# Second product of both MLPs as Strassen's seven products of halves

## The chip, the cores and the metric

The kernel runs on one core of one Trainium2 chip. The metric is device time in microseconds of one execution. A core has five engines that run their own instruction queues in order: TensorE (matmuls, PE in the profile, with PEld for its weight loads), VectorE (DVE), ScalarE (ACT), GpSimd (POOL) and SyncE (SP, which here only issues transfers). SBUF is the on-chip memory of 128 partitions; PSUM holds what TensorE accumulates, in banks of 512 float32 columns per partition.

## The reference

Two transformer blocks over 512 tokens of width 1024, in float32. The first has a hybrid mixer (gated spatial mixing and a gated delta rule), cross attention to 256 memory rows and an MLP; the second has an mLSTM and sliding window attention with gates, an MLP, and a gated per-layer embedding. What matters here are the two MLPs:

```
def squared_relu_mlp(h, w1, w2):                 # block 1: w1 1024x4096, w2 4096x1024
    return jnp.square(jax.nn.relu(h @ w1)) @ w2
...
u = rmsnorm_2(x, norm_mlp_g[i]) @ w_up[i]        # block 2, the same sizes
x = x + jnp.square(jax.nn.relu(u)) @ w_down[i]
```

## The kernel before

**Layout.** Activations are kept feature-major: a tile is 128 features by 512 tokens. The residual `x` is `self.x`, [128, 8, 512], and stays in SBUF. Other large operands lie in numbered slots `S0` to `S12` of 8 KB per partition (`slot`, line 86): 0 to 8 in a pool that lives through the whole kernel, 9 to 12 in one opened for a part of it.

**Precision.** Every float32 product is three matmuls (`mm3`, line 217). Each operand is split in a high part, rounded by ScalarE, and a low part, the rest, subtracted by VectorE (`split_sb` line 257, for weights `wload` line 193, the two instructions of which are lines 203 and 204); high x high, high x low and low x high are accumulated in the same PSUM bank.

**Weights.** A granule is 256 output columns of 1024 input rows. `wgran` (line 207) loads it in two halves of [128, 4, 256], 512 KB each, over SP (line 200) into `wr` (two buffers), and splits them into `wh` and `wl` (three buffers each), all in the pool `wp` that is opened at line 70 and never closed. The layout on the host (`gran`, line 311) makes each half one contiguous piece per partition.

**Product.** `proj_fm` (line 224) takes a granule and for each of its two output tiles runs 8 x 3 matmuls with a 128x128 weight tile as the stationary operand and 512 token columns as the moving one, into one of three PSUM banks `psd`, and calls a function that evacuates the bank. `proj_tm` exchanges the roles: 256 weight columns move.

**The MLP.** `ffn` (line 792) divides the 4096 hidden features in four quarters. `up(q)` makes eight hidden tiles with four granules of the first weight: VectorE applies relu and the norm's factor (line 804), ScalarE squares (line 805), and the tile is split into its high and low slots (lines 261 and 262). `down(q)` takes four granules of the second weight and adds to `x` (`add_res`, line 401). The order is up(0), up(1), down(0), up(2), down(1), up(3), down(2), down(3), with two sets of four slots for the hidden tiles. In the last quarter the evacuation also prepares the next stage, tile by tile: a scaled split of `x` (lines 264 and 265) and sums of squares, squared by ScalarE and added by GpSimd (line 276), one such sum after the second MLP and two after the first (`between`, line 829; `tail`, line 1184).

**Order.** The program is written as data flow over tiles in pools. A planner puts each engine's instructions in a fixed order beforehand: by their place in the program, but an instruction whose inputs and buffers are expected to be ready may go ahead of one that still waits. It adds the semaphores. A pool that is closed gives its memory to pools opened later; pools are placed one above another.

Of the kernel before, what the change touches and what calls it, by code (L numbers as in the profile page):

```python
# [2 lines left out]

# [1 line left out]

# [59 lines left out]
class Kern:  # L65
    def __init__(self, tc, ctx, D, out, dbg=None):
        self.tc, self.nc, self.ctx, self.D, self.out = tc, tc.nc, ctx, D, out
        self.dbg = dbg or {}
        self.const = ctx.enter_context(tc.tile_pool(name="const", bufs=1))
        self.wp = ctx.enter_context(tc.tile_pool(name="wp", bufs=3))  # L70
        self.sp = ctx.enter_context(tc.tile_pool(name="sp", bufs=1))
        self.tp = ctx.enter_context(tc.tile_pool(name="tp", bufs=2))
        self.pd = ctx.enter_context(tc.tile_pool(name="pd", bufs=3, space=PSUM))
        self.ps = ctx.enter_context(tc.tile_pool(name="ps", bufs=1, space=PSUM))
        self.n = 0
# [8 lines left out]


    def slot(self, i, shape, dt=F32):
        return (self.sp if i < 9 else self.sp2).tile(shape, dt, tag=f"S{i}", name=self.uid(f"S{i}"))

    def t(self, pool, shape, tag, dt=F32, bufs=None):
# [82 lines left out]
    def softplus(self, pool, z, n, tag):  # L172
# [16 lines left out]
        nc.vector.scalar_tensor_tensor(out=a, in0=a, scalar=2.0, in1=s, op0=ALU.mult, op1=ALU.add)  # L189
        return a  # L190


    def wload(self, src, kt, n, pieces=None):

# [19 lines left out]
        lo = [parts[k // 4][1][:, k % 4] for k in range(nk)]  # L214
        return hi, lo

    def mm3(self, ps, ah, al, bh, bl, first, last):

        mm = self.nc.tensor.matmul
        mm(ps, ah, bh, start=first, stop=False)  # L220
        mm(ps, ah, bl, start=False, stop=False)  # L221
        mm(ps, al, bh, start=False, stop=last)  # L222

    def proj_fm(self, w, xh, xl, tiles, evac, ncol=T, pool=None):
        wh, wl = w
# [500 lines left out]
    def xattn(self, xh, xl, acc, mem):  # L726
        nc = self.nc
        kh, kl, vh, vl = mem
        rs = self.tok_rs(acc, "rs")
        ident = self.mask("ident")  # L730
        oh, ol = [], []
        with self.tc.tile_pool(name="xa", bufs=2) as xp, self.psums() as self.pc:
# [4 lines left out]
            for h in range(4):  # L737
                q = self.slot((0, 1, 7, 4)[h], [P, 4, T], F32R)
# [7 lines left out]
                for t2 in range(2):  # L746
                    ps = self.psc("sc").rearrange("p (i m) -> p i m", i=2)
                    for i in range(2):
                        c = slice((2 * t2 + i) * P, (2 * t2 + i + 1) * P)
# [5 lines left out]
                    p = self.t(xp, [P, 2, 256], "p")  # L755
# [23 lines left out]
        xh, xl = self.pair((9, 10)), self.pair((11, 12))  # L779
        acc = self.new_acc()  # L780

        def ev(o, ps):
# [6 lines left out]
        return xh, xl, acc  # L789


    def ffn(self, w1, w2, xh, xl, acc, evac):
        nc = self.nc
        rs = self.tok_rs(acc, "rs")
        bc = self.tok_bc(rs, "bc")
        H = {}

        def up(q):
            s = (0, 1, 2, 3) if q % 2 == 0 else (4, 5, 6, 7)
            hh, hl = self.pair(s[:2]), self.pair(s[2:])  # L800

            def ev(o, ps):
                t = self.t(self.tp, [P, T], "e1")
                nc.vector.scalar_tensor_tensor(out=t, in0=ps, scalar=0.0, in1=bc, op0=ALU.max, op1=ALU.mult)  # L804
                nc.scalar.activation(t, t, AF.Square)  # L805
                self.split_sb(hh[o], hl[o], t)

            for g in range(4):
                self.proj_fm(self.wgran(w1, 4 * q + g), xh, xl, (2 * g, 2 * g + 1), ev)
            H[q] = hh, hl  # L810

        def down(q, ev):
            for g in range(4):
                self.proj_fm(self.wgran2(w2, 4 * q + g), *H[q], (2 * g, 2 * g + 1), ev)

        up(0)
        up(1)
        down(0, self.add_res)
        up(2)
        down(1, self.add_res)  # L820
        up(3)
        down(2, self.add_res)
        down(3, evac)

    def wgran2(self, name, g):
        return self.wgran(name, g)


    def between(self):

        nc = self.nc
        g12 = self.t(self.tp, [P, KT], "g12", bufs=1)
        c1, c2 = VCOL["norm_final"], VCOL["norm_mix_g_2"]
        nc.vector.tensor_tensor(out=g12, in0=self.vec[:, c1:c1 + 8], in1=self.vec[:, c2:c2 + 8], op=ALU.mult)
        xh, xl = self.pair((0, 1)), self.pair((2, 3))
        acc, acc2 = self.new_acc(), None

        def ev(o, ps):
            nonlocal acc2
            if o == 0:  # L840
                acc2 = self.slot(9, [P, T])
            self.add_res(o, ps)
            self.split_sb(xh[o], xl[o], self.x[:, o], g12[:, o:o + 1])
            self.sq_acc(acc, self.x[:, o], o)
            self.sq_acc(acc2, self.x[:, o], o, scale=self.vcol("norm_final", o))

        def fin():
            self.dump("x3", self.x)
            r1 = self.tok_rs(acc, "rs")
# [333 lines left out]

    def tail(self):
        nc = self.nc
        xh, xl = self.pair((0, 1)), self.pair((2, 3))
        acc = self.new_acc()

        def ev(o, ps):
            self.add_res(o, ps)  # L1190
            self.norm_tile(o, xh, xl, acc, "norm_ple_g_2")

        def ple():
            self.dump("x6", self.x)
            raw = self.slot(9, [P, 2, T])
            nc.sync.dma_start(raw, self.D["p"])
            ph = self.slot(10, [P, 4, T], F32R)
            for i in range(2):
                self.split_sb(ph[:, i], ph[:, 2 + i], raw[:, i])
            pp = [self.slot(i, [P, 4, T]) for i in (11, 12)]  # L1200

            def ev_p(o, ps):
                nc.scalar.copy(pp[o // 4][:, o % 4], ps)
# [27 lines left out]
            sq = self.slot(9, [P, 2, 2, 256])  # L1231
            y = self.slot(10, [P, 2, 1024])
            one = self.ones[:, 0:1]
            with self.psums() as self.pc:

# [18 lines left out]
                r0 = stat(0)  # L1254
# [12 lines left out]
                ps = self.pss()  # L1267
# [13 lines left out]
def body(tc, D, out, dbg=None):  # L1281
    with ExitStack() as ctx:
        K = Kern(tc, ctx, D, out, dbg)
        K.setup()
        K.mixer()
        mem = K.memory()
        with tc.tile_pool(name="sp2", bufs=1) as K.sp2:
            op = K.w_out1()
            op = K.xattn(*op, mem)
            ev, fin = K.between()  # L1290
            K.ffn("ffn_w1", "ffn_w2", *op, ev)
            op2 = fin()
        mh, ml = K.mixer2(*op2)
        with tc.tile_pool(name="sp3", bufs=1) as K.sp2:
            xh, xl = K.pair((9, 10)), K.pair((11, 12))
# [8 lines left out]
            K.dump("x5", K.x)  # L1304
            ev, ple = K.tail()
            K.ffn("w_up_2", "w_down_2", xh, xl, acc, ev)
            ple()


# [1 line left out]
def gran(w, n=256):  # L1311

    kk, nn = w.shape
    return np.ascontiguousarray(w.reshape(kk // 512, 4, P, nn // n, n).transpose(3, 0, 2, 1, 4))


def fm(a):
# [8 lines left out]
def layout(i):  # L1326
# [21 lines left out]
        o["w_ple_gate" if n == "w_ple_gate_2" else n] = gran(sq(n))  # L1348
    for n in ("ffn_w2", "w_down_2"):
        w = sq(n)  # L1350
        o[n] = np.ascontiguousarray(np.concatenate([gran(w[1024 * q:1024 * q + 1024]) for q in range(4)], axis=0))
# [31 lines left out]
```

## Time and profile before

| | us |
|---|---|
| median of 3 runs (lowest, highest) | 1758.17 (1754.64, 1764.05) |
| the profiled execution | 1758.89 |
| its span, first to last instruction | 1757.1 |
| TensorE busy, matmuls | 1719.7 (8740 instructions) |
| VectorE busy | 1011.4 (2039) |
| ScalarE busy | 720.9 (1254) |
| GpSimd busy | 148.4 (126) |

The granted TensorE clock was 0.992 over the span. Busy times of successive instructions overlap: a matmul of 512 columns is shown with 0.39 us, while the next starts 0.23 us after it. So a price of TensorE or VectorE work is read from the distance between starts. The two MLPs take about 0.36 ms each: the evacuations of `up` (line 804) run from 461.2 to 1594.7 us over both, and the first MLP's weights are loaded from 432.3 us on, its last tile of `x` added at 811.1 us. A row of the timeline holds the start, the duration, the engine, the line, the operation, output and input, and in brackets how long the engine stood idle before it and what ended that. A row of the table by stage holds for each stretch its length and then busy time and count of PE, PEld, DVE, ACT and POOL, the granted clock, the DMA share and GB/s.

### The profile page before, as it was taken

The page shows a single profiled execution, that of the slowest core. Times are in us where ns is not written, and L with a number is a line of the kernel's source. Part 1 is how long each engine was busy: PE and PEld are TensorE (multiplying, and loading weights), DVE is VectorE, ACT ScalarE, POOL GpSimd, SP SyncE. Part 2 cuts the span into 40 slices and gives each one's busy share as a digit, 9 for nine tenths or more (in the row PEclk, how much of TensorE's full clock was granted, in tenths as well). Part 3 has the DMA queues.
Part 4 walks back from the last instruction along what each step waited for, and adds up shares of the span by engine and source line. Part 5 has one row for each costly group of instructions (what it writes and reads, how often), then busy time and mean ns, then how long its engine had stood idle before and what let it go on. Part 6 is the DMA issues. An engine that isn't in the chain of part 4 may idle for free.

```text
span 1757.1 us, 22629 instructions
## 1 busy us (share of the span) xinstructions
PE 1719.7 (98%) x8740; PEld 1427.2 (81%) x8740; DVE 1011.4 (58%) x2039; ACT 720.9 (41%) x1254; POOL 148.4 (8%) x126
## 2 busy tenths in 40 slices
PE   7999999999999999999999999999999999999997
PEld 6987788877888888888888887788888888888886
DVE  6898886655543444446755469865555434344446
ACT  5344444444333333334444448654234323232343
POOL 2211321201000000012000000000120000000112
PEclk9999998999999999999999999999999999999999
DMA  5221232312222223223222321223222222323231
GB/s 196 88 72 61 71 97 77 118 51 72 96 97 96 93 89 95 95 86 95 73 73 74 95 73 49 72 73 96 86 97 89 91 95 96 96 96 108 90 102 61
DMA packets 49436, 155.09 MB, mean 88 GB/s; under 512 B 9392, under 2 KB 11696, under 8 KB 49328
## 3 DMA queue, kind: packets, MB, share of 16 engines
q1 hardware_dynamic: 49328, 153.64, 27.4%
q8 instruction: 69, 1.13, 0.3%
q14 instruction: 39, 0.32, 0.1%
HBM read 151.26 MB, written 2.10 MB: 87 GB/s over the span
## 4 chain that ended last, share of the span: by engine, by line
PE 87%; DVE 9%; ACT 2%; issue 2%; DMA 0%; POOL 0%; SPq 0%; DVEq 0%; ACTq 0%
PE psd L221 26%; PE psd L222 26%; PE psd L220 26%; DVE wl L204 1%; PE c L563 1%; ACT wh L203 1%; PE lg L1147 1%; PE po L1174 1%; PE c L512 1%; PE m L1068 1%; DVE S L368 1%; DVE e L319 1%; PE pss L1169 0%; PE m L1076 0%; DVE dA L583 0%
## 5 line engine op out<-in xcount | busy, mean ns | idle before, releaser
L220 PE MATMUL psd<-S,wh 128*128 128x512 f32 (+1 forms) x1968 | 770.5, 392 | 6.3 <-ACT wh L203 6.3
L222 PE MATMUL psd<-S,wl 128*128 128x512 f32 (+1 forms) x1968 | 774.3, 394 | 1.3 <-DVE wl L204 1.3
L221 PE MATMUL psd<-S,wh 128*128 128x512 f32 (+1 forms) x1904 | 748.1, 393 | 2.4 <-DVE S L265 2.3
L204 DVE TENSOR_TENSOR wl<-wr,wh 128x1024 fp32r<-128x1024 f32 (+3 forms) x281 | 349.4, 1243 | 227.0 <-ACT wh L203 225.9
L203 ACT CAST wh<-wr 128x1024 fp32r<-128x1024 f32 (+3 forms) x281 | 292.0, 1039 | 434.3 <-PE psd L221 406.5
L220 PEld LDWEIGHTS psd<-S,wh 128*128 128x128 f32 x1968 | 372.7, 189 | 86.2 <-ACT wh L203 7.2
L222 PEld LDWEIGHTS psd<-S,wl 128*128 128x128 f32 x1968 | 371.5, 189 | 79.8 <-DVE wl L204 2.3
L221 PEld LDWEIGHTS psd<-S,wh 128*128 128x128 f32 x1904 | 358.7, 188 | 80.6 <-DVE S L265 4.2
L276 POOL TENSOR_TENSOR acc<-acc,sq 128x512 f32<-128x512 f32 (+1 forms) x47 | 67.9, 1446 | 916.8 <-ACT sq L274 916.3
L401 DVE TENSOR_TENSOR x_fm<-psd,x_fm 128x512 f32<-128x512 f32 x88 | 60.7, 690 | 137.8 <-PE psd L222 137.7
L221 PE MATMUL psd<-wl,S 128*128 128x256 f32 (+2 forms) x480 | 137.4, 286 | 0.6 <-DVE wl L204 0.6
L222 PE MATMUL psd<-wh,S 128*128 128x256 f32 (+2 forms) x480 | 137.1, 286 | 0.0
L220 PE MATMUL psd<-wh,S 128*128 128x256 f32 (+2 forms) x480 | 136.5, 284 | 0.0
L804 DVE SCALAR_TENSOR_TENSOR e<-psd,bc 128x512 f32<-128x512 f32 x64 | 44.3, 691 | 112.2 <-PE psd L222 109.3
L805 ACT ACTIVATE e<-e 128x512 f32<-128x512 f32 x64 | 40.4, 632 | 135.1 <-DVE e L804 135.1
L221 PEld LDWEIGHTS psd<-wl,S 128*128 128x128 f32 x480 | 91.6, 191 | 1.4 <-DVE wl L204 1.0
L220 PEld LDWEIGHTS psd<-wh,S 128*128 128x128 f32 x480 | 91.8, 191 | 0.4
L222 PEld LDWEIGHTS psd<-wh,S 128*128 128x128 f32 x480 | 91.8, 191 | 0.1
L262 DVE TENSOR_TENSOR S<-e,S 128x512 fp32r<-128x512 f32 (+1 forms) x84 | 56.7, 675 | 49.2 <-ACT S L261 49.2
L261 ACT CAST S<-e 128x512 fp32r<-128x512 f32 (+1 forms) x84 | 50.5, 601 | 42.9 <-POOL e L931 27.1
L264 ACT ACTIVATE S<-x_fm,vec 128x512 fp32r<-128x512 f32 x40 | 28.9, 721 | 55.4 <-DVE x_fm L401 36.9
L319 DVE SCALAR_TENSOR_TENSOR e<-e,vec,e 128x511 f32<-128x511 f32 (+2 forms) x60 | 46.6, 779 | 2.6 <-ACT e L316 2.2
(411 smaller groups left out, 1459.7 us busy)
## 6 DMA issues: line engine op xcount, KB each, us to landing
wr<-in_ffn_w_dram SPq DMA_DIRECT2D x64, 512.0 KB
wr<-in_w_up_dram SPq DMA_DIRECT2D x32, 512.0 KB
wr<-in_w_down_dram SPq DMA_DIRECT2D x32, 512.0 KB
wr<-in_w_in_qk_dram SPq DMA_DIRECT2D x16, 512.0 KB
wr<-in_w_in_v_dram SPq DMA_DIRECT2D x12, 512.0 KB
wr<-in_xa_wk_dram SPq DMA_DIRECT2D x8, 512.0 KB
wr<-in_xa_wv_dram SPq DMA_DIRECT2D x8, 512.0 KB
wr<-in_xa_wq_dram SPq DMA_DIRECT2D x8, 512.0 KB
```

The lines of the kernel that those rows point to most:

```text
L203: nc.scalar.copy(hi[:, c], raw[:, c])
L204: nc.vector.tensor_tensor(out=lo[:, c], in0=raw[:, c], in1=hi[:, c].bitcast(F32), op=ALU.subtract)
L220: mm(ps, ah, bh, start=first, stop=False)
L221: mm(ps, ah, bl, start=False, stop=False)
L222: mm(ps, al, bh, start=False, stop=last)
L261: nc.scalar.copy(hi, src)
L262: nc.vector.tensor_tensor(out=lo, in0=src, in1=hi.bitcast(F32), op=ALU.subtract)
L276: eng.tensor_tensor(out=acc, in0=acc, in1=sq, op=ALU.add)
L319: nc.vector.scalar_tensor_tensor(out=c[:, s:], in0=xr[:, :T - s], scalar=w(j), in1=c[:, s:], op0=ALU.mult, op1=ALU.add)
L401: self.nc.vector.tensor_tensor(out=self.x[:, o], in0=ps, in1=self.x[:, o], op=ALU.add)
L804: nc.vector.scalar_tensor_tensor(out=t, in0=ps, scalar=0.0, in1=bc, op0=ALU.max, op1=ALU.mult)
L805: nc.scalar.activation(t, t, AF.Square)
```

## The change

`down` no longer multiplies a granule as a whole. The granule's 1024 x 256 weights are four blocks, two halves of the input tiles (even and odd ones) by two halves of the output columns; the hidden quarter is likewise two halves of the features by two halves of the tokens (256 each). Strassen's scheme in Winograd's form computes the four blocks of the result with seven products of such halves instead of eight, each of 4 x 3 matmuls with 256 moving columns. It needs four sums of weight blocks and four sums of hidden blocks, each split like any operand.

- `st_weights` loads the four raw blocks in three transfers, makes the four sums on VectorE and splits seven blocks, in three pieces of 1024 columns and one of 512.
- `st_fill` is called after each `up` granule: it makes the four hidden sums on VectorE (`ms`), and splits seven pieces of 256 columns in four steps. `st_operand` takes seven slots for them.
- `st_gemm` runs the seven products in the PSUM banks X, Z (a new pool of four banks, `px`) and Y (a bank of `psd`), and adds after each product to the block of `x` that needs it: products 3, 5 and 6 accumulate on top of what is in X, product 4 on Z.
- `ffn` runs the quarters in the order up(0), down(0), up(1), down(1), and so on. After a granule of the last quarter `post` does for its two tiles what the evacuation did before.
- The weight pool is no longer one: `weights()` opens it with three buffers for everything else and with five for each MLP (the second to the end of the kernel). Slots are renumbered to fit (`perm`), and a pool `fp` holds what is used in an MLP only. `halves` lays the second weights out on the host, without arithmetic.

```
-        self.wp = ctx.enter_context(tc.tile_pool(name="wp", bufs=3))
...
+    @contextmanager
+    def weights(self, bufs=3):
+        with self.tc.tile_pool(name=self.uid("wp"), bufs=bufs) as self.wp:
+            yield
...
+    def st_fill(self, H, k, e1, e2):
...
+        h = (slice(0, 256), slice(256, 512))
+        ms = self.t(self.fp, [P, 4, 256], "ms", bufs=1)
+        TT(out=ms[:, 3], in0=e2[:, h[1]], in1=e1[:, h[1]], op=ALU.subtract)
+        TT(out=ms[:, 1], in0=e1[:, h[0]], in1=e1[:, h[1]], op=ALU.subtract)
+        STT(out=ms[:, 2], in0=ms[:, 3], scalar=-1.0, in1=e1[:, h[0]], op0=ALU.mult, op1=ALU.subtract)
+        STT(out=ms[:, 0], in0=ms[:, 2], scalar=-1.0, in1=e2[:, h[0]], op0=ALU.mult, op1=ALU.subtract)
+        self.split_sb(t[6][:, 0, k], t[6][:, 1, k], e1[:, h[0]])
+        self.split_sb(t[4][:, :, k], t[5][:, :, k], e2.rearrange("p (a c) -> p a c", a=2))
+        self.split_sb(t[2][:, :, k], t[3][:, :, k], ms[:, 2:4])
+        self.split_sb(t[0][:, :, k], t[1][:, :, k], ms[:, 0:2])
...
+    def st_weights(self, src):
...
+        nc.sync.dma_start(r0, src[:, 0:2])
+        nc.sync.dma_start(r1, src[:, 2:3])
+        nc.sync.dma_start(r2, src[:, 3:4])
...
+        split(r0)
+        nc.vector.tensor_tensor(out=ss[:, 0], in0=r0[:, 0], in1=r2[:, 0], op=ALU.add)
+        nc.vector.tensor_tensor(out=ss[:, 1], in0=r1[:, 0], in1=r2[:, 0], op=ALU.add)
+        split(ss)
+        s2 = self.t(self.wp, [P, 2, T], "ws2", bufs=1)
+        nc.vector.tensor_tensor(out=s2[:, 0], in0=ss[:, 0], in1=r1[:, 0], op=ALU.add)
+        nc.vector.tensor_tensor(out=s2[:, 1], in0=s2[:, 0], in1=r0[:, 1], op=ALU.add)
+        split(s2)
+        split(r1)
+        a11, a12, s3, s1, s2, s4, a22 = out
+        return a11, a12, s1, s2, s4, s3, a22
+
+    def st_gemm(self, src, H, o1, post):
...
+        def prod(i, ps, m, first):
+            ah, al = w[i]
+            for k in range(4):
+                c = slice(k * P, (k + 1) * P)
+                self.mm3(ps, ah[:, c], al[:, c], hi[m][:, k], lo[m][:, k], first and k == 0, k == 3, not first)
+
+        def add(n, t, ps, op=ALU.add):
+            TT(out=x[n][t], in0=x[n][t], in1=ps, op=op)
+
+        prod(0, X, 0, True)
+        add(0, 0, X)
+        prod(1, Y, 1, True)
+        add(0, 0, Y)
+        prod(2, Z, 4, True)
+        add(1, 1, Z, ALU.subtract)
+        prod(3, X, 5, False)
+        add(0, 1, X)
+        prod(4, Z, 2, False)
+        add(0, 1, Z)
+        prod(5, X, 6, False)
+        add(1, 1, X, ALU.subtract)
+        prod(6, X, 3, False)
+        add(1, 0, X, ALU.subtract)
+        for o in (o1, o1 + 1):
+            post(o)
...
+            for q in range(4):
+                H = None
+                for g in range(4):
...
+                    self.proj_fm(self.wgran(w1, 4 * q + g), xh, xl, (2 * g, 2 * g + 1), ev)
+                    H = H or self.st_operand(slots)
+                    self.st_fill(H, g, *es)
+                for g in range(4):
+                    self.st_gemm(self.D[w2][4 * q + g], H, 2 * g, post if q == 3 else lambda o: None)
...
-        K.setup()
...
+        with K.weights():
+            K.setup()
+            K.mixer()
+            mem = K.memory()
...
+        with K.weights(5), tc.tile_pool(name="fp", bufs=1) as K.fp:
+            K.sp2 = K.fp
             ev, fin = K.between()
...
+            K.ffn("ffn_w1", "ffn_w2", *op, (0, 1, 4, 7, 8, 9, 10), ev)
             op2 = fin()
...
+        with K.weights():
+            K.perm = [2, 3, 5, 6, 0, 1, 4, 7, 8]
+            mh, ml = K.mixer2(*op2)
...
+        with K.weights(5), tc.tile_pool(name="fp", bufs=1) as K.fp:
...
+            K.ffn("w_up_2", "w_down_2", xh, xl, acc, (2, 3, 5, 6, 8, 9, 10), ev)
```

More of the change, by code (lines that the diff above doesn't have):

```diff
@@ L1 @@
 import math
-from contextlib import ExitStack
+from contextlib import ExitStack, contextmanager
 import numpy as np
@@ L215, in wgran, with mm3 @@
         return hi, lo
-    def mm3(self, ps, ah, al, bh, bl, first, last):
+    def mm3(self, ps, ah, al, bh, bl, first, last, more=False):
         mm = self.nc.tensor.matmul
-        mm(ps, ah, bh, start=first, stop=False)
-        mm(ps, ah, bl, start=False, stop=False)
-        mm(ps, al, bh, start=False, stop=last)
+        mm(ps, ah, bh, start=first, stop=False, skip_group_check=more)
+        mm(ps, ah, bl, start=False, stop=False, skip_group_check=more)
+        mm(ps, al, bh, start=False, stop=last, skip_group_check=more)
     def proj_fm(self, w, xh, xl, tiles, evac, ncol=T, pool=None):
@@ L778, in xattn @@
                     ol.append(O[:, 2 + o])
-        xh, xl = self.pair((9, 10)), self.pair((11, 12))
+        xh, xl = self.pair((2, 3)), self.pair((5, 6))
         acc = self.new_acc()
@@ L789, in xattn @@
         return xh, xl, acc
-    def ffn(self, w1, w2, xh, xl, acc, evac):
-        nc = self.nc
[L794 to L823, printed above, removed]
@@ new lines, in st_weights, with split @@
+    def st_weights(self, src):
+        nc = self.nc
+        r0 = self.t(self.wp, [P, 2, T], "wr", bufs=2)
+        r1 = self.t(self.wp, [P, 1, T], "wr1", bufs=2)
+        ss = self.t(self.wp, [P, 2, T], "ws", bufs=1)
+        r2 = self.t(self.wp, [P, 1, T], "wr2", bufs=2)
+        nc.sync.dma_start(r0, src[:, 0:2])
+        nc.sync.dma_start(r1, src[:, 2:3])
+        nc.sync.dma_start(r2, src[:, 3:4])
+        out = []
+        def split(raw):
+            n = raw.shape[1]
+            hi, lo = self.t(self.wp, [P, n, T], "wh", F32R), self.t(self.wp, [P, n, T], "wl", F32R)
+            self.split_sb(hi, lo, raw)
+            out.extend((hi[:, i], lo[:, i]) for i in range(n))
+        split(r0)
[9 more added lines that the diff above has]
+        return a11, a12, s1, s2, s4, s3, a22
@@ new lines, in st_gemm @@
+    def st_gemm(self, src, H, o1, post):
+        nc = self.nc
+        TT = nc.vector.tensor_tensor
+        w = self.st_weights(src)
+        _, hi, lo = H
+        X, Z = (self.t(self.px, [P, T], "x")[:, :256] for _ in range(2))
+        Y = self.psd()[:, :256]
+        x = [[self.x[:, o1 + n, t * 256:t * 256 + 256] for t in range(2)] for n in range(2)]
+        def prod(i, ps, m, first):
[21 more added lines that the diff above has]
+            post(o)
@@ L834, in between, with ev @@
         nc.vector.tensor_tensor(out=g12, in0=self.vec[:, c1:c1 + 8], in1=self.vec[:, c2:c2 + 8], op=ALU.mult)
[L835 to L839, printed above, removed]
+        ops = None
+        def ev(o):
+            nonlocal ops
             if o == 0:
-                acc2 = self.slot(9, [P, T])
-            self.add_res(o, ps)
+                ops = self.pair((2, 3)), self.pair((5, 6)), self.new_acc(), self.t(self.fp, [P, T], "acc2", bufs=1)
+            xh, xl, acc, acc2 = ops
             self.split_sb(xh[o], xl[o], self.x[:, o], g12[:, o:o + 1])
@@ L1185, in tail, with ev @@
         nc = self.nc
[L1186 to L1191, printed above, removed]
+        raw = self.t(self.fp, [P, 2, T], "p", bufs=1)
+        nc.sync.dma_start(raw, self.D["p"])
+        ops = None
+        def ev(o):
+            nonlocal ops
+            if o == 0:
+                ops = self.pair((0, 1)), self.pair((4, 7)), self.new_acc()
+            self.norm_tile(o, *ops, "norm_ple_g_2")
         def ple():
+            xh, xl, acc = ops
             self.dump("x6", self.x)
-            raw = self.slot(9, [P, 2, T])
-            nc.sync.dma_start(raw, self.D["p"])
-            ph = self.slot(10, [P, 4, T], F32R)
+            ph = self.slot(8, [P, 4, T], F32R)
             for i in range(2):
                 self.split_sb(ph[:, i], ph[:, 2 + i], raw[:, i])
-            pp = [self.slot(i, [P, 4, T]) for i in (11, 12)]
+            pp = [self.slot(i, [P, 4, T]) for i in (2, 3)]
             def ev_p(o, ps):
@@ L1230, in ple @@
             wh, wl = self.wgran("w_ple_gate", 3)
[L1231 to L1232 removed]
+            sq = self.slot(5, [P, 2, 2, 256])
+            y = self.slot(6, [P, 2, 1024])
             one = self.ones[:, 0:1]
@@ L1283, in body @@
         K = Kern(tc, ctx, D, out, dbg)
-        K.setup()
[L1285 to L1289, printed above, removed]
+        with K.weights():
+            K.setup()
+            K.mixer()
+            mem = K.memory()
+            with tc.tile_pool(name="sp2", bufs=1) as K.sp2:
+                op = K.w_out1()
+                op = K.xattn(*op, mem)
+        with K.weights(5), tc.tile_pool(name="fp", bufs=1) as K.fp:
+            K.sp2 = K.fp
             ev, fin = K.between()
-            K.ffn("ffn_w1", "ffn_w2", *op, ev)
+            K.ffn("ffn_w1", "ffn_w2", *op, (0, 1, 4, 7, 8, 9, 10), ev)
             op2 = fin()
-        mh, ml = K.mixer2(*op2)
-        with tc.tile_pool(name="sp3", bufs=1) as K.sp2:
-            xh, xl = K.pair((9, 10)), K.pair((11, 12))
+        with K.weights():
+            K.perm = [2, 3, 5, 6, 0, 1, 4, 7, 8]
+            mh, ml = K.mixer2(*op2)
+            K.perm = list(range(13))
+            xh, xl = K.pair((0, 1)), K.pair((4, 7))
             acc = K.new_acc()
@@ L1314, in gran, with halves @@
     return np.ascontiguousarray(w.reshape(kk // 512, 4, P, nn // n, n).transpose(3, 0, 2, 1, 4))
+def halves(w):
+    v = w.reshape(4, 2, P, -1, 2, P).transpose(3, 2, 4, 1, 0, 5).reshape(-1, P, 4, 4 * P)
+    return v[:, :, [0, 1, 3, 2]]
 def fm(a):
@@ L1350, in layout @@
         w = sq(n)
-        o[n] = np.ascontiguousarray(np.concatenate([gran(w[1024 * q:1024 * q + 1024]) for q in range(4)], axis=0))
+        o[n] = np.ascontiguousarray(np.concatenate([halves(w[1024 * q:1024 * q + 1024]) for q in range(4)], axis=0))
     w = sq("w_in_2")
```

25 lines of the change are left out of this document (22 added, 3 removed).

## The prediction

> **What bounds the kernel now.** I read the page's busy line first, then the chain that ended last, then a table by stage, then single rows of the timeline.
>
> ```profile
> PE 1719.7 (98%) x8740; PEld 1427.2 (81%) x8740; DVE 1011.4 (58%) x2039; ACT 720.9 (41%) x1254; POOL 148.4 (8%) x126
> ...
> PE psd L221 26%; PE psd L222 26%; PE psd L220 26%; DVE wl L204 1%; PE c L563 1%; ACT wh L203 1%; PE lg L1147 1%; PE po L1174 1%; PE c L512 1%; PE m L1068 1%; DVE S L368 1%; DVE e L319 1%; PE pss L1169 0%; PE m L1076 0%; DVE dA L583 0%
> ```
>
> The three matmul lines of `mm3` hold 78% of the chain. Two stretches of four granules show the MLP: an `up` (476 to 520.8 us) and a `down` (640 to 684.8 us).
>
> ```profile
> 476.00:520.80 44.80, 44.80 (x194) 36.23 (x193) 20.74 (x24) 18.05 (x24) 0.00 (x0) 1.00 0.29 94
> 640.00:684.80 44.80, 44.80 (x194) 36.24 (x194) 15.37 (x17) 9.65 (x10) 0.00 (x0) 1.00 0.30 95
> ```
>
> TensorE never stops; VectorE (third pair) is busy 15.37 of 44.80 us in `down`. So the stage costs what TensorE issues, and the next two views give the price of that: second tiles of two successive `down` granules, then 256-column matmuls, first and last of 12 and of 21.
>
> ```profile
> 649.33 0.69 DVE L401 TENSOR_TENSOR x_fm<-psd,x_fm 128x512 f32<-128x512 f32 x1 [3.50 <-PE psd L222]
> 660.48 0.69 DVE L401 TENSOR_TENSOR x_fm<-psd,x_fm 128x512 f32<-128x512 f32 x1 [3.50 <-PE psd L222]
> ```
>
> ```profile
> 239.73 0.28 PE L222 MATMUL psd<-S,wl 128*128 128x256 f32 x1
> 241.04 0.28 PE L221 MATMUL psd<-S,wh 128*128 128x256 f32 x1
> ...
> 303.22 0.28 PE L221 MATMUL psd<-wl,S 128*128 128x256 f32 x1
> 305.60 0.28 PE L220 MATMUL psd<-wh,S 128*128 128x256 f32 x1
> ```
>
> A granule of 48 matmuls of 512 columns takes 11.15 us, 0.232 us each. At 256 columns they start 1.31/11 = 0.119 us apart, and 2.38/20 = 0.119 in the second stretch, each with its own weight load.
>
> **The change, part by part.**
>
> *Term 1, the products.* Per granule 48 matmuls become 7 x 4 x 3 = 84 of 256 columns: 84 x 0.119 = 10.0 us for 11.15. There are 32 such granules: 32 x 1.15 = **-37 us**. This all lies on the path, if VectorE and ScalarE keep up.
>
> *VectorE's load.* Its cost is the start-to-start step, not the duration:
>
> ```profile
> 238.22 1.21 DVE L204 TENSOR_TENSOR wl<-wr,wh 128x1024 fp32r<-128x1024 f32 x1
> 239.36 0.15 DVE L168 SCALAR_TENSOR_TENSOR drt<-drt,dss 128x8 f32<-128x8 f32 x1
> ...
> 241.35 0.42 DVE L709 TENSOR_TENSOR e<-psd,bc 128x256 f32<-128x256 f32 x1
> 241.69 0.16 DVE L529 TENSOR_TENSOR dkd<-ds,ee 128x4 f32<-128x4 f32 x1
> 241.76 0.69 DVE L540 TENSOR_TENSOR slg<-slg,ds 128x512 f32<-128x512 f32 x1
> 242.36 0.56 DVE L543 TENSOR_TENSOR kdec<-c,dkd 128x384 f32<-128x384 f32 x1
> ```
>
> 1.14, 0.34 and 0.60 us for 1024, 256 and 512 columns. A changed `down` granule has three splits of 1024 and one of 512 (4.0), four sums of 512 (2.4) and seven additions of 256 (2.4): 8.8 us, beside 10.0 of TensorE. It fits with 1.2 us to spare, where before it had seven. [...] ScalarE is busy 9.65 of 44.80 us in `down` (fourth pair above) and gets three and a half casts per granule where it had two: under 5 us. An `up` granule gets four sums of 256 and 768 more columns to split (1.4 + 0.9 us) beside the 20.74/4 = 5.2 it has now, inside 11.2: nothing, with that much TensorE work to cover it.
>
> *Term 2, the weight pools.* Before, `wp` lives through the whole kernel, and the next stage's weights are fetched long ahead:
>
> ```profile
> 432.31 35.35 SPq L200 DMA_DIRECT2D wr<-in_ffn_w_dram  x7
> ...
> 452.43 0.69 DVE L401 TENSOR_TENSOR x_fm<-psd,x_fm 128x512 f32<-128x512 f32 x1 [0.69 <-PE psd L222]
> ```
>
> The first MLP load is issued at 432 us, 20 us before the stage in front of it adds its last tile. Afterwards the pool is closed and opened again at three places (before the first MLP, before `mixer2`, before the second MLP), at the same address. I take it that the first load into a new pool waits until the last matmul on the old one is done. No row shows such a reopened pool; the nearest rows are loads with nobody ahead of them, and the start of the kernel:
>
> ```profile
> 306.80 0.33 SPq L200 DMA_DIRECT2D wr<-in_w_out_b_dram  x1
> ...
> 310.30 1.05 ACT L203 CAST wh<-wr 128x1024 fp32r<-128x1024 f32 x1 [1.39 <-DMA wr<-in_w_out_b_dram]
> ```
>
> ```profile
> 5.27 0.80 PE L220 MATMUL psd<-S,wh 128*128 128x512 f32 x1 [5.27 <-ACT wh L203]
> ...
> 6.79 0.63 PE L220 MATMUL psd<-S,wh 128*128 128x512 f32 x1
> 7.21 0.63 PE L221 MATMUL psd<-S,wh 128*128 128x512 f32 x1
> 7.64 0.63 PE L222 MATMUL psd<-S,wl 128*128 128x512 f32 x1
> ```
>
> A 512 KB load takes 3.5 us from issue to the cast, the cast 1.05; with 0.4 for the last matmul to end TensorE stands still about 4.8 us, and some 0.5 more for the low half. After standing 5.27 us its matmuls start 0.43 apart instead of 0.23, for about 4 us: 0.2 x 9 = 1.8 more. Together 7 us, three times: **+21 us**. Queued behind the waiting load on SP are only later weights. Ends: 0, if the memory comes free tile by tile; 31, if the second 512 KB (another 3.4 us at the same rate) is waited for as well. I take 21, which the rows price.
>
> *Term 3, from `up` to `down`.* Before, `up(1)` stood between `up(0)` and `down(0)`; now each `down` reads operands that the `up` just ended has to fill.
>
> ```profile
> 682.29 0.39 PE L222 MATMUL psd<-S,wl 128*128 128x512 f32 x1
> ...
> 682.72 0.69 DVE L804 SCALAR_TENSOR_TENSOR e<-psd,bc 128x512 f32<-128x512 f32 x1 [3.49 <-PE psd L222]
> ...
> 683.45 0.63 ACT L805 ACTIVATE e<-e 128x512 f32<-128x512 f32 x1 [5.47 <-DVE e L804]
> 684.11 0.62 ACT L261 CAST S<-e 128x512 fp32r<-128x512 f32 x1
> ...
> 684.76 0.69 DVE L262 TENSOR_TENSOR S<-e,S 128x512 fp32r<-128x512 f32 x1 [1.35 <-ACT S L261]
> ```
>
> From the last matmul's start to the low half is 3.16 us, 2.9 after the slot of the next one; the sums `ms` can add 0.4. Product 0 needs only the first tile (12 x 0.119 = 1.4), product 1 three of its four steps (1.1). Some 0.7 us stays open: 8 x 0.7 = **+6 us**; ends 0 (other products in between) and 8 x 1.9 = 15 (only product 0 covers).
>
> *Term 4, the shared banks.* Products 3, 5 and 6 accumulate in X and 4 in Z, each behind an addition that reads the bank. Between 5 and 6 lies none of this granule's, so the planner must put the next granule's product 0 (1.4 us) there. The addition starts 0.43 after the last matmul and takes 0.42, but one VectorE split can be ahead of it (1.14): about 0.2 us late in the 24 granules that term 5 does not take, **+5 us**. Ends: 0, and 32 x 0.8 = 25 if nothing is put between.
>
> *Term 5, the last quarter of each MLP.* There VectorE also splits x: two more of 512, 10.0 us in all. Pool adds beside it, and slows it:
>
> ```profile
> 797.90 2.10 DVE L204 TENSOR_TENSOR wl<-wr,wh 128x1024 fp32r<-128x1024 f32 x1 [1.39 <-ACT wh L203]
> ```
>
> ```profile
> 797.63 1.29 POOL L276 TENSOR_TENSOR S<-S,sq 128x512 f32<-128x512 f32 x1
> ```
>
> ```profile
> L204 DVE TENSOR_TENSOR wl<-wr,wh 128x1024 fp32r<-128x1024 f32 (+3 forms) x281 | 349.4, 1243 | 227.0 <-ACT wh L203 225.9
> ```
>
> 2.10 instead of a mean of 1.24, 0.86 lost to a Pool addition. Four of those per granule in the first MLP, two in the second; at an estimated 0.6 each, since not every one meets such an operation, VectorE needs 12.4 and 11.2 us for 10.0. Three granules of each pay (the fourth's work falls behind the stage): 7.2 + 3.6 = **+11 us**; ends 0, and 3 x (3.4 + 1.7) = 15 at the full 0.86.
>
> Nothing else: the same 1 MB per granule, in three transfers instead of two, DMA at 0.30; SP issues at 0.33 us each. `slot` renames memory only, and `p` is fetched earlier.
>
> Sum: -37 + 21 + 6 + 5 + 11 = +6 us on the profiled execution of 1758.89 us, which is 0.7 above the median of 1758.17: **1765 us**, 0.4% more. About 0.5% (8.8 us) is what can be told from no change.
>
> **The rivals.**
>
> *Faster, no gap at the pools.* If each new tile waits only for the memory under it, `wr` is free as soon as its split is done, and term 2 is 0: 1765 - 21 = **1744 us**. For it: 20 us of lead in the rows of term 2. Against: the pools are opened and closed as wholes, and the high and low halves of the new one lie where the last stage's are still being read.
>
> *Slower, VectorE sets the pace.* At durations instead of steps a granule costs 3 x 1.24 + 5 x 0.69 + 7 x 0.42 = 10.1, and 15 hand-overs of 0.04 (682.68 to 682.72, above) make 10.7: TensorE waits 0.7 us in 32 granules, +22, with term 4 inside it and term 5 up by 3: 1765 + 22 - 5 + 3 = **1785 us**. It decides once the 15 operations take over 10.0 us, 14% above my 8.8. For it: waits of a queue that runs in order, in a plan fixed beforehand; against: the steps above.
>
> *The halves are not cheaper.* If a matmul could not start faster than its weight load, 84 loads at 189 ns make 15.9 us:
>
> ```profile
> L220 PEld LDWEIGHTS psd<-S,wh 128*128 128x128 f32 x1968 | 372.7, 189 | 86.2 <-ACT wh L203 7.2
> ```
>
> +4.7 x 32 = 150, **1915 us**. The steps of 0.119 speak against it.
>
> **How the numbers follow.** Mine 0.43, with its own range 1754 to 1782, half of the way to the ends of terms 3 to 5, which will not all lie on one side (level 0.21, slower 0.22); no gap 0.30 (faster 0.24, level 0.06); VectorE 0.24, slower; loads 0.03, slower. So faster 0.24, same 0.27, slower 0.49. The range 1738 to 1796 spans the first three cases with the ends of their terms.
>
> **What would show it.** Term 1: runs of 256-column matmuls 0.119 us apart in the MLPs. Term 2: three gaps of about 5 us at the reopened pools, the first load issued only after the last matmul, and 0.43 us steps behind. Terms 3 to 5: waits of TensorE on VectorE, a share of VectorE near nine tenths in `down`, and gaps that grow in the last quarter. No gaps at the pools, or a VectorE that is full with TensorE waiting in each granule, makes the prediction wrong.

## The result and the profile after

The changed kernel takes 1769.12 us (median of 8 runs) where the kernel before takes 1759.73 in the runs beside it: 1.0043 times as long, with a 95% interval of 1.0022 to 1.0064. One of the eight took 2669.79 us, at a granted clock of 0.573; the ratio leaves it out. The forecast was 1765 us, 0.4% more. The profiled execution of the changed kernel takes 1768.61 us, its span 1766.7.

The page of the changed kernel: busy time by engine, and the chain that ended last.

```profile
PE 1711.3 (97%) x9892; PEld 1472.0 (83%) x9892; DVE 1264.3 (72%) x2583; ACT 802.2 (45%) x1382; POOL 149.2 (8%) x126
...
PE 81%; DVE 12%; ACT 3%; issue 2%; DMA 1%; POOL 0%; SPq 0%; DVEq 0%; ACTq 0%
PE psd L228 20%; PE psd L227 19%; PE psd L229 19%; PE x L227 5%; PE x L228 4%; PE x L229 4%; DVE wl L211 2%; DVE S L272 1%; PE c L570 1%; ACT wh L210 1%; DVE wl L269 1%; PE lg L1233 1%; PE po L1260 1%; DVE x_fm L872 1%; PE c L519 1%
```

TensorE is still the chain, but VectorE now holds 12% of it (9% before), and VectorE's busy time has grown by 253 us. Next the timeline of the changed kernel at the first reopened pool (line 207 issues the weight loads, 291 is the sum of squares with ones, 227 to 229 are the three matmuls of `mm3`).

```profile
424.67 8.42 SPq L207 DMA_DIRECT2D wr<-in_xa_wo_dram  x2
455.70 0.81 SPq L207 DMA_DIRECT2D wr<-in_ffn_w_dram  x2
```

```profile
455.28 0.40 PE L229 MATMUL psd<-S,wl 128*128 128x512 f32 x1
458.60 1.05 PE L291 MATMUL pss<-ones,acc 128*128 128x1 f32 x8 [2.93 <-DVE acc L283]
460.63 0.80 PE L227 MATMUL psd<-S,wh 128*128 128x512 f32 x1 [0.97 <-ACT wh L210]
461.22 0.63 PE L228 MATMUL psd<-S,wh 128*128 128x512 f32 x1
461.65 0.63 PE L227 MATMUL psd<-S,wh 128*128 128x512 f32 x1
462.07 0.63 PE L228 MATMUL psd<-S,wh 128*128 128x512 f32 x1
```

The first MLP load is issued at 455.70 us, just after the last matmul on the old pool ended; before, that load went out 20 us ahead. The next product starts 5.35 us after the last one, and its matmuls are 0.43 us apart instead of 0.23. In the rows, 2.93 us of the stop is a wait for VectorE's sum of squares and only 0.97 a wait for weights. But the chain that ended last at this place goes by the load and its cast (start, length, what); the wait for the sum runs beside them:

```profile
455.70 3.75 DMA wr<-in_ffn_w_dram
459.53 1.05 ACT wh L210
460.63 0.80 PE psd L227
```

At the other two reopened pools the next product starts 6.84 and 5.15 us after the last one, and there the chain goes by the sum of squares: the first cast behind the second pool is done at about 817.8 us, the product starts at 819.73.

Busy time in four stretches of the changed kernel: a Strassen `down`, an `up`, a `down`, and the `down` of the last quarter of the first MLP (columns as in the table by stage: length, then PE, weight loads, VectorE, ScalarE, GpSimd).

```profile
593.50:636.20 42.70, 42.66 (x344) 41.42 (x342) 35.51 (x59) 17.48 (x20) 0.00 (x0) 1.00 0.34 102
636.20:679.60 43.40, 43.40 (x189) 34.96 (x188) 31.09 (x50) 19.29 (x29) 0.00 (x0) 1.00 0.30 96
679.60:722.20 42.60, 42.60 (x343) 41.40 (x342) 35.52 (x59) 17.45 (x20) 0.00 (x0) 1.00 0.33 101
765.60:813.00 47.40, 42.30 (x337) 40.54 (x335) 41.99 (x61) 25.44 (x37) 19.74 (x14) 1.00 0.06 21
```

In the inner `down` VectorE is 83% busy and TensorE does not stop. In the last one VectorE is 89% busy, GpSimd runs for 19.74 us, and TensorE stands idle for 5.1 of 47.4 us. Who is waited for there:

```profile
PE x L227 <- DVE x_fm L872: 4.0, 4, 2.2
PE pss L291 <- DVE acc L283: 2.7, 1, 2.7
PE x L227 <- ACT sq L281: 1.1, 1, 1.1
```

TensorE waits for VectorE's additions to `x`, which have to read a bank before it is used again. The first and the third row make up the 5.1 us; the 2.7 us for the sum of squares fall behind the stretch.

### The profile page after: what moved, and what is told of

It is laid out like the page before. It is cut to its first block, busy times and chain, and to the rows that moved or that the text cites. A ratio compares the mean times of both kernels' runs of the same rounds, so it can differ in the third digit from the quotient of the medians.

```text
span 1766.7 us, 25613 instructions
## 1 busy us (share of the span) xinstructions
PE 1711.3 (97%) x9892; PEld 1472.0 (83%) x9892; DVE 1264.3 (72%) x2583; ACT 802.2 (45%) x1382; POOL 149.2 (8%) x126
## 4 chain that ended last, share of the span: by engine, by line
PE 81%; DVE 12%; ACT 3%; issue 2%; DMA 1%; POOL 0%; SPq 0%; DVEq 0%; ACTq 0%
PE psd L228 20%; PE psd L227 19%; PE psd L229 19%; PE x L227 5%; PE x L228 4%; PE x L229 4%; DVE wl L211 2%; DVE S L272 1%; PE c L570 1%; ACT wh L210 1%; DVE wl L269 1%; PE lg L1233 1%; PE po L1260 1%; DVE x_fm L872 1%; PE c L519 1%
## 5 line engine op out<-in xcount | busy, mean ns | idle before, releaser
L227 PE MATMUL psd<-S,wh 128*128 128x512 f32 (+1 forms) x1584 | 612.4, 387 | 7.4 <-ACT wh L210 6.5
L229 PE MATMUL psd<-S,wl 128*128 128x512 f32 (+1 forms) x1584 | 608.8, 385 | 1.3 <-DVE wl L211 1.3
L228 PE MATMUL psd<-S,wh 128*128 128x512 f32 (+1 forms) x1520 | 585.9, 386 | 0.8 <-DVE S L272 0.7
L211 DVE TENSOR_TENSOR wl<-wr,wh 128x1024 fp32r<-128x1024 f32 (+4 forms) x217 | 269.1, 1240 | 143.7 <-ACT wh L210 143.0
L227 PEld LDWEIGHTS psd<-S,wh 128*128 128x128 f32 x1584 | 302.1, 191 | 65.4 <-ACT wh L210 7.5
L228 PEld LDWEIGHTS psd<-S,wh 128*128 128x128 f32 x1520 | 289.7, 191 | 57.9 <-DVE S L269 2.3
L210 ACT CAST wh<-wr 128x1024 fp32r<-128x1024 f32 (+4 forms) x217 | 224.7, 1036 | 220.3 <-PE psd L228 111.7
L227 PE MATMUL x<-S,wh 128*128 128x256 f32 x768 | 218.6, 290 | 8.6 <-DVE x_fm L872 7.3
L228 PE MATMUL x<-S,wh 128*128 128x256 f32 x768 | 215.5, 282 | 0.0
L229 PE MATMUL x<-S,wl 128*128 128x256 f32 x768 | 212.9, 282 | 0.0
L227 PEld LDWEIGHTS x<-S,wh 128*128 128x128 f32 x768 | 144.1, 190 | 16.7 <-DVE x_fm L872 11.1
L228 PEld LDWEIGHTS x<-S,wh 128*128 128x128 f32 x768 | 146.1, 190 | 0.4
L229 PEld LDWEIGHTS x<-S,wl 128*128 128x128 f32 x768 | 144.9, 190 | 0.0
L227 PEld LDWEIGHTS psd<-wh,S 128*128 128x128 f32 x480 | 91.7, 191 | 0.4
```

What stands on the lines that cost most here:

```text
L210: nc.scalar.copy(hi[:, c], raw[:, c])
L211: nc.vector.tensor_tensor(out=lo[:, c], in0=raw[:, c], in1=hi[:, c].bitcast(F32), op=ALU.subtract)
L227: mm(ps, ah, bh, start=first, stop=False, skip_group_check=more)
L228: mm(ps, ah, bl, start=False, stop=False, skip_group_check=more)
L229: mm(ps, al, bh, start=False, stop=last, skip_group_check=more)
```

## The experiments

The theory at this point: reopening the weight pools costs about 21 us and so takes back more than half of what the seven products save; VectorE is short only in the last quarters. The rivals: the pools are hidden, or VectorE sets the pace everywhere.

### The kernel before, with its weight pool reopened

```diff
-        self.wp = ctx.enter_context(tc.tile_pool(name="wp", bufs=3))
+        self.reopen("wp0")      # closes self.wp, if there is one, and opens it again
...
+            K.reopen("wp1")
             ev, fin = K.between()
...
             op2 = fin()
+            K.reopen("wp2")
...
+            K.reopen("wp3")
             ev, ple = K.tail()
```

`reopen` opens the pool with three buffers, as before, and with `side="right"`.

> The kernel before with one edit: its pool of weights is closed and opened again, at the same address and with the same three buffers, before the first MLP, before mixer2 and before the second MLP. No arithmetic changes. My theory (a reopened pool waits for the last matmul on the old one, term 2): three idle gaps of TensorE of 4 to 5.5 us, 0.43 us steps behind each, 18 to 21 us over the kernel before, a ratio of about 1.011. Rival (the reopening is hidden, and what the change loses it loses to VectorE): within 3 us of the kernel before. In the plan of this kernel the sum-of-squares matmuls at the three places also stand right behind the last product, where the kernel before has them some 16 matmuls further on; so part of the gap, 2.9 us, may be this order and not the load.

Measured: 1780.99 us, 1.012 of the kernel before (1.0093 to 1.0147), that is 21 us more (16 to 26). TensorE in its timeline at the first place:

```profile
450.58 0.39 PE L230 MATMUL psd<-S,wl 128*128 128x512 f32 x1
453.89 1.45 PE L292 MATMUL pss<-ones,acc 128*128 128x1 f32 x8 [2.93 <-DVE acc L284]
455.77 0.79 PE L228 MATMUL psd<-S,wh 128*128 128x512 f32 x1 [0.43 <-ACT wh L211]
456.36 0.63 PE L229 MATMUL psd<-S,wh 128*128 128x512 f32 x1
456.79 0.63 PE L228 MATMUL psd<-S,wh 128*128 128x512 f32 x1
```

So the price of term 2 stands without any Strassen product: a stop of 5.2 us, with matmuls 0.43 us apart behind it, and stops at all three places (the second, with two sums in it, is 7.2 us). Yet the reopening did two things. It delayed the loads, and it moved the sum-of-squares matmuls in the plan to the place right behind the last product, where they wait 2.93 us for VectorE. In the kernel before they stand 16 matmuls further on, and the wait is covered:

```profile
455.95 0.96 PE L284 MATMUL pss<-ones,acc 128*128 128x1 f32 x8
```

### The changed kernel, memory handed over tile by tile

```diff
-        with self.tc.tile_pool(name=self.uid("wp"), bufs=bufs) as self.wp:
+        with self.tc.tile_pool(name=self.uid("wp"), bufs=bufs, reuse_waits="tile") as self.wp:
```

> The changed kernel with one edit: a tile in a reopened pool of weights waits only for the earlier users of its own bytes, not for those of the whole old pool. The order of the instructions on every engine stays as in the changed kernel. If the wait of the first load is all of term 2: the first loads go out about 20 us before the stage ahead ends, the gaps go, and the time falls by 18 to 21 us to about 1750, 0.995 of the kernel before. [...] Rival (VectorE): nothing changes, 1769.

Measured: 1767.41 us, 1.0047 of the kernel before (1.0030 to 1.0064): no different from the changed kernel. As a number that is what the rival, VectorE, had forecast; the rows show another reason. SP, TensorE and the VectorE row that ends the second wait, at the first place:

```profile
436.11 8.63 SPq L207 DMA_DIRECT2D wr<-in_ffn_w_dram  x2
```

```profile
455.79 0.40 PE L229 MATMUL psd<-S,wl 128*128 128x512 f32 x1
459.12 1.05 PE L291 MATMUL pss<-ones,acc 128*128 128x1 f32 x8 [2.93 <-DVE acc L283]
460.03 0.48 PE L227 MATMUL psd<-S,wh 128*128 128x512 f32 x1
...
462.96 0.80 PE L229 MATMUL psd<-S,wl 128*128 128x512 f32 x1 [1.44 <-DVE wl L211]
```

```profile
461.60 0.17 DVE L169 SCALAR_TENSOR_TENSOR rst<-rst,rsv 128x4 f32<-128x4 f32 x1
461.68 1.23 DVE L211 TENSOR_TENSOR wl<-wr,wh 128x1024 fp32r<-128x1024 f32 x1
```

The load now goes out at 436.11 us, 19.7 us ahead of the last product, and nothing is won. The order on every engine is that of the changed kernel, the one that the reopening alone had brought about in the first experiment: TensorE still meets the sum of squares first (2.93 us), and VectorE still has the chain of the norm ahead of the low half of the weights (1.44 us). An early load does not help behind such an order. The first matmul on the low half starts 7.17 us after the last product (455.79 to 462.96); in the changed kernel it was 7.22 (455.28 to 462.50). So the load that waits, term 2, and the fixed order run side by side, and the order alone produces a stop as long. The opposite case, the old order with late loads, was not tried; that the load alone would hold TensorE as long follows only from the chain of the changed kernel, at the first place.

### The changed kernel, one weight pool throughout

```diff
-        with K.weights(5), tc.tile_pool(name="fp", bufs=1) as K.fp:
+            with tc.tile_pool(name="fp", bufs=1) as K.fp:   # inside the one K.weights()
...
-            hi, lo = self.t(self.wp, [P, n, T], "wh", F32R), self.t(self.wp, [P, n, T], "wl", F32R)
+            if summed:
+                hi, lo = (self.t(self.fp, [P, n, T], i, F32R, bufs=2) for i in ("vh", "vl"))
+            else:
+                hi, lo = self.t(self.wp, [P, n, T], "wh", F32R), self.t(self.wp, [P, n, T], "wl", F32R)
...
-        r2 = self.t(self.wp, [P, 1, T], "wr2", bufs=2)
+        r2 = self.t(self.fp, [P, 1, T], "wr2", bufs=1)
```

> The changed kernel with one pool of weights through the whole kernel (three buffers); the raw blocks, the sums and two more buffers for the split sums come from the pool that each MLP opens for itself, and one raw block has one buffer instead of two. Both the wait and the order at the three places become those of the kernel before. My theory: minus 18 to 21 us, about 1750, a ratio of 0.995 to the kernel before (0.993 to 0.997). Rival (VectorE sets the pace, the pools are hidden): within 3 us of the changed kernel, a ratio of 1.004. The three gaps of about 5 us should be gone from the trace; the small waits inside the MLPs stay as they were.

Measured: 1753.35 us, 0.9974 of the kernel before (0.9957 to 0.9992): faster than both kernels, 12 us (7 to 17) under the changed one by the ratios. SP and TensorE at the first place, then the stretch of the last `down` of the first MLP:

```profile
430.93 22.70 SPq L207 DMA_DIRECT2D wr<-in_ffn_w_dram  x5
```

```profile
454.22 0.40 PE L229 MATMUL psd<-S,wl 128*128 128x512 f32 x1
454.45 0.40 PE L227 MATMUL psd<-S,wh 128*128 128x512 f32 x1
454.69 0.96 PE L291 MATMUL pss<-ones,acc 128*128 128x1 f32 x8
455.51 0.47 PE L228 MATMUL psd<-S,wh 128*128 128x512 f32 x1
```

```profile
755.00:805.00 50.00, 44.45 (x329) 42.19 (x328) 44.40 (x60) 25.64 (x36) 16.67 (x11) 0.93 0.19 58
```

The sum of squares stands inside the next products again and waits for nothing. Only 12 of the 21 us came back, because the last quarters grew: from the first Strassen matmul to the last, the first MLP takes 309.9 us where the changed kernel takes 305.4, the second 308.9 for 305.3. Over the steps of 0.119, TensorE loses 11.1 and 10.4 us in the last `down` of the two; in the changed kernel it loses 7.5 and 6.5, its final wait for the sum not counted. Two things are new in the first MLP's. With the pool open, VectorE splits two blocks of the next stage's weights there as well (at 800.04 and 803.21 us). And the granted clock in the row above is 0.93, where it was 1.00 in the changed kernel: 0.07 of 50 us, 3.5 us, is most of the growth, while TensorE's idle time is 5.55 us for 5.10. In this execution the stretch holds a stop of 2.2 us; in the changed kernel's first MLP a stop as long (2.16 us, up to 795.69) left the clock at 1.00. In the second MLP both kernels split such weights, and the clock is 0.93 for 0.96. How much of the growth is the clock's chance in one execution is not shown.

### No sums of weights

```diff
-        nc.vector.tensor_tensor(out=ss[:, 0], in0=r0[:, 0], in1=r2[:, 0], op=ALU.add)
-        nc.vector.tensor_tensor(out=ss[:, 1], in0=r1[:, 0], in1=r2[:, 0], op=ALU.add)
-        split(ss)
-        s2 = self.t(self.wp, [P, 2, T], "ws2", bufs=1)
-        nc.vector.tensor_tensor(out=s2[:, 0], in0=ss[:, 0], in1=r1[:, 0], op=ALU.add)
-        nc.vector.tensor_tensor(out=s2[:, 1], in0=s2[:, 0], in1=r0[:, 1], op=ALU.add)
-        split(s2)
+        split(r0)
+        split(r0)
```

> The changed kernel without the four sums of weight blocks: the raw blocks are split and multiplied in their place, so the output is not the reference's; all products, splits and additions to x stay. VectorE does 2.4 us less of its 8.8 us per granule of the second product. My theory (it fits beside 10.0 us of TensorE except in the last quarters): the small waits of the first three quarters, about 1.4 us each, fall by at most half, the last quarters lose most of their 6 and 4 us, in all minus 5 to 12 us against the changed kernel, 1757 to 1764. Rival (VectorE sets the pace in every granule): minus 20 us or more, under 1750. If sums cost nothing at all: 1769.

Measured: 1760.22 us, 1.0004 of the kernel before (0.9988 to 1.0021), some 7 us (2 to 12) under the changed kernel. An inner `down` and the last `down` of the first MLP:

```profile
591.50:631.40 39.90, 39.86 (x326) 39.07 (x325) 28.60 (x48) 16.45 (x19) 0.00 (x0) 1.00 0.28 88
763.70:807.00 43.30, 41.62 (x337) 40.39 (x335) 34.37 (x53) 25.49 (x37) 18.89 (x14) 1.00 0.07 23
```

The inner `down` is as full of TensorE work as with the sums; the last one has lost most of its idle time (1.7 us for 5.1). From the first Strassen matmul to the last, each MLP is 3.9 us shorter (301.6 and 301.4 us), and this sits in its last quarter. VectorE does not set the pace of a granule; the rival's 20 us are not there.

### No additions of squares in the last quarters

```diff
-            eng.tensor_tensor(out=acc, in0=acc, in1=sq, op=ALU.add)
+            if self.add_sq or k == KT - 1:      # False while a last quarter's tiles are finished
+                eng.tensor_tensor(out=acc, in0=acc, in1=sq, op=ALU.add)
```

> The changed kernel without GpSimd's additions of squares in the last quarter of both MLPs (six of each sum of eight; the squares themselves, the first and the last step stay), so the norm behind is wrong. In its profile TensorE waits 6.2 and about 4 us in these two quarters. My theory (term 5: GpSimd's additions slow VectorE by 0.6 us each, four per granule in the first MLP and two in the second): the waits go almost wholly, minus 7 to 10 us, 1759 to 1762. Rival (VectorE's own splits and sums fill it, GpSimd only happens beside them): minus 0 to 3 us, 1766 to 1769.

Measured: 1752.68 us, 0.9965 of the kernel before (0.9947 to 0.9983), 14 us (9 to 19) under the changed kernel by the ratios, where 7 to 10 were expected. Between the same points the MLPs take 299.6 and 300.4 us, 5.8 and 4.9 less. VectorE's groups in the last `down` of the first MLP, first in the changed kernel, then here (line 272 is the low half of the scaled `x`, 269 that of a weight block, 872 an addition to `x`; all three lines stand one or two further down here):

```profile
L872 DVE TENSOR_TENSOR x_fm<-x_fm,x 128x256 f32<-128x256 f32 x23 | 9.2, 413 | 2.4 <-PE x L229 2.4
L269 DVE TENSOR_TENSOR wl<-ws,wh 128x1024 fp32r<-128x1024 f32 x6 | 8.9, 1475 | 0.2 <-ACT wh L268 0.2
L272 DVE SCALAR_TENSOR_TENSOR S<-x_fm,g,S 128x512 fp32r<-128x512 f32 x7 | 8.1, 1157 | 0.8 <-ACT S L271 0.8
```

```profile
L874 DVE TENSOR_TENSOR x_fm<-x_fm,x 128x256 f32<-128x256 f32 x23 | 9.3, 416 | 3.7 <-PE x L230 3.6
L270 DVE TENSOR_TENSOR wl<-ws,wh 128x1024 fp32r<-128x1024 f32 x6 | 7.3, 1220 | 0.2 <-ACT wh L269 0.2
L273 DVE SCALAR_TENSOR_TENSOR S<-x_fm,g,S 128x512 fp32r<-128x512 f32 x7 | 5.2, 747 | 0.8 <-ACT S L272 0.8
```

GpSimd's additions stretch these two operations, which take both tensors from SBUF, 747 to 1157 ns and 1220 to 1475; the additions that take one of them from PSUM take 413 ns beside GpSimd and 416 without. Why the two kinds differ is not shown.

### One pool, and no additions of squares

The edit of the last section on the kernel with one pool.

> The kernel with one pool of weights through the whole kernel, and without GpSimd's additions of squares in the last quarter of both MLPs, so the norm behind is wrong. In the one-pool kernel the last quarters are 3 and 4 us longer than in the changed kernel, since the next stage's weights are split there as well. If GpSimd's additions are the larger part of what holds VectorE up: minus 8 to 14 us against the one-pool kernel (1753), 1739 to 1745. If VectorE's own work is the larger part: minus 0 to 6 us, 1747 to 1753.

Measured: 1736.47 us, 0.9875 of the kernel before (0.9850 to 0.9901), 17 us (12 to 23) under the one-pool kernel by the ratios, where 8 to 14 were expected. The MLPs fall to 300.0 and 301.5 us between the same points. So nearly the whole loss of the last quarters needs both: a VectorE that is nearly full (without the sums the loss went too), and GpSimd beside it.

### One pool, last quarter with the plain product

```diff
-            for q in range(4):
+            for q in range(3):
...
+            for g in range(4):
+                self.proj_fm(self.wgran(w1, 12 + g), xh, xl, (2 * g, 2 * g + 1), ev_h)
+            for g in range(4):
+                self.proj_fm(self.wgran(w2 + "p", g), hh, hl, (2 * g, 2 * g + 1), ev_x)
```

> The kernel with one pool of weights through the whole kernel, and the last quarter of both MLPs with the plain second product of the kernel before (four granules of 48 matmuls of 512 columns), the other three quarters as Strassen. If the last quarter of the one-pool kernel is held up by VectorE (46.6 and 48.6 us and some more for the 40.0 us that its products issue): a plain quarter takes 44.6 us with VectorE far from full, 3 to 6 us less each, minus 6 to 11 us in all, about 1744, a ratio of 0.991 to the kernel before. If the last quarter is held up by something that the form of the product doesn't touch: plus 9 us, 1762.

Measured: 1740.74 us, 0.9902 of the kernel before (0.9878 to 0.9926), 13 us (7 to 18) under the one-pool kernel by the ratios, where 6 to 11 were expected. The last `down` of each MLP:

```profile
755.00:800.00 45.00, 45.00 (x195) 36.25 (x193) 23.26 (x24) 22.61 (x32) 17.13 (x14) 1.00 0.29 94
1620.00:1665.00 45.00, 45.00 (x195) 36.23 (x194) 20.34 (x25) 17.12 (x25) 8.82 (x6) 1.00 0.26 79
```

GpSimd works as before, VectorE is half empty, TensorE does not stop. The product with fewer multiplications is slower in this one quarter, and the kernel that leaves it out there is the fastest complete one here.

## Why the prediction was right, and where its reasons were not

- *Term 1, the products (-37)*: right. Down the inner quarters the matmuls start 0.119 us apart:

```profile
507.45 0.28 PE L227 MATMUL x<-S,wh 128*128 128x256 f32 x1
...
508.76 0.28 PE L229 MATMUL x<-S,wl 128*128 128x256 f32 x1
```

  Twelve matmuls, 1.31/11. The rival of halves that are not cheaper is out.
- *Term 2, the weight pools (+21)*: the size is right (21 by the first experiment), and the late load, the stop of 5 us and the steps of 0.43 are as described. The reason was half of it. At the first place the sum "load 3.5, cast 1.05, end of the matmul 0.4" is the chain that ended last, with 3.75 for the load. What it missed is that the reopening reorders the plan: a wait of 2.93 us for the sum of squares runs beside the load, is enough for a stop as long, and ends last at the other two places. So that the three stops came out near the forecast length was in part luck. The step that failed is "if the memory comes free tile by tile, term 2 is 0": the memory did come free tile by tile in the second experiment, and the term stayed. What removes it is a pool that is not reopened.
- *Terms 3 and 4 (+11)*: about right. A quarter, `up` and `down`, takes 86.0 us here (593.50 to 679.57 to 765.58), where its matmuls at 0.232 and 0.119 make 84.6:

```profile
593.50 0.28 PE L227 MATMUL x<-S,wh 128*128 128x256 f32 x1
679.57 0.28 PE L227 MATMUL x<-S,wh 128*128 128x256 f32 x1
765.58 0.28 PE L227 MATMUL x<-S,wh 128*128 128x256 f32 x1
```

  That is 1.4 us in each of six inner quarters, 8.5 in all, spread over some 14 waits of 0.04 to 0.2 us, mostly where one product hands over to the next. The split between the two terms, 6 and 5, was not: the hand-over from `up` to `down` holds about 0.3 us of it per quarter, where 0.7 was forecast (the forecast's own figures, 2.9 + 0.4 - 1.4 - 1.1, give 0.8).
- *Term 5, the last quarters (+11)*: the mechanism was right, the size low: 7.5 and 6.5 us, 14 in all, where 7.2 and 3.6 were forecast. The first MLP was met. In the second, GpSimd has half the additions to make, but TensorE lost nearly as much; about 1.7 of its 6.5 us are half rate, which the forecast did not count (granted clock 0.96 over these 47.45 us, 0.57 from 1675 to 1679).
- *The sum*: -37 + 21 + 8.5 + 14 = +6.5 us; the ratio says 7.6 (3.9 to 11.3).
- *The rivals.* "VectorE sets the pace" fell: without the sums the kernel gains 7 us, in the last quarters. It counted every operation with its whole duration and 0.04 us of hand-over. That does not hold for every operation (the split at 461.68 us in the second experiment starts 0.08 us after the start of one shown with 0.17), and the inner `down`, in which TensorE stands still for under 0.1 of 42.7 us, is not paced by VectorE. "No gap at the pools" was priced at 1744; with one pool it is 1753, because 7.5 us of the gap come back in the last quarters, part of it as half rate. That coupling of terms 2 and 5 was missing from the prediction. "The halves are not cheaper" is out by term 1, and was also priced wrongly: 150 us over the kernel before were added to 1765, in which term 1's saving of 37 already stands; 1952 would follow.
- The 9.7 us between the two profiled executions are not the price of the change alone: about 6 lie in `deltanet`, in the first mixer, which the change does not touch (last section).

## What to carry to other kernels

Closing and opening a pool costs more than the wait of its first load: it changes the order planned around it, so look at what stands first in each queue behind the boundary, and keep a pool that feeds the busiest engine open. When a trade moves work from the bound engine to one that had room, check the stretch where that engine has the least room, and leave the trade out there. Additions on GpSimd are not free for VectorE: here they slowed operations of it on two SBUF tensors (747 to 1157 ns, 1220 to 1475).

## What was not expected of the hardware

In `deltanet` (first mixer), which the change does not touch, the same stop of TensorE, 1.66 us by the trace, leaves the clock alone in one execution and halves it in another. First the kernel before, then the changed one, each with the matmul behind the stop and the 5 us that follow (granted clock third from the end):

```profile
242.97 1.16 PE L512 MATMUL c<-dq,dk 128*128 128x128 f32 x8 [1.65 <-DVE kdec L543]
```

```profile
245.00:250.00 5.00, 5.00 (x46) 5.00 (x45) 3.35 (x7) 2.17 (x5) 1.45 (x2) 1.00 0.05 5
```

```profile
240.18 1.16 PE L519 MATMUL c<-dq,dk 128*128 128x128 f32 x8 [1.66 <-DVE kdec L550]
```

```profile
245.00:250.00 5.00, 5.00 (x25) 5.00 (x25) 2.07 (x5) 1.67 (x3) 1.28 (x1) 0.50 0.07 7
```

The half clock lasts from about 242 to 255.6 us although TensorE is busy all that time by its rows: the granted clock over these 13.6 us is 0.50 in the changed kernel's execution and 1.00 in that of the kernel before. From that stop to the next long one pass 37.1 us instead of 30.7. The two stops are as long (1.65 and 1.66 us), so their length does not decide. What in the activity of this stage brings the half clock on, and what keeps it for some 14 us, stays open.
